# A hybrid block kernel: two weight loads on ScalarE's queue, a norm's sums one product earlier, weight sums stored by GpSimd, and a set VectorE order in the last half

## The chip, the cores and the metric

The kernel runs on one core of one Trainium2 chip. Time is device microseconds of one execution of the whole program, with all inputs and outputs in the chip's HBM. Lower is better. Before the change, three runs took 2157.55, 2159.38 and 2161.64 us; the median is 2159.38.

## What is computed

One residual block over a sequence of 2048 frames with 1024 channels, all in float32 (a depth of 1):

```python
def rmsnorm(x, g):
    return x * lax.rsqrt(jnp.mean(x * x, axis=-1, keepdims=True) + EPS) * g

def reference(x, ...):
    h = rmsnorm(x, norm_mix_pre)
    u_pool, u_glu, g_a, g_b = jnp.split(h @ w_in, [512, 1536, 2560], axis=-1)   # 1024 -> 3584
    branch_a = pool_mixer(u_pool, pool_w, pool_scale, w_pool_out)   # windows 2, 4, 8, 16; 512 -> 1024
    branch_b = conformer_conv(u_glu, conv_w, conv_b, ln_g, ln_b, w_conv_out)
    # GLU, causal depthwise conv of 31 taps, LayerNorm, swish, 512 -> 1024
    merged = sigmoid(g_a) * branch_a + sigmoid(g_b) * branch_b
    x = x + rmsnorm(merged @ w_o, norm_mix_post)
    h = rmsnorm(x, norm_mlp_pre)
    f = jnp.square(relu(h @ w_up)) @ w_down                          # 1024 -> 4096 -> 1024
    return x + rmsnorm(f, norm_mlp_post)
```

## The kernel before

**Layout and blocks.** Channels lie on the 128 partitions, frames on the free axis. The 2048 frames are two blocks of 1024 (`NB`), each of two halves of 512 frames (`T`); a tile of 128 x 1024 float32 (512 KB) holds one half for two groups of 128 channels. The stages run one after the other on TensorE: input projection of block 0 (`glu`, `pool`, `ga`, `gb`), branch A of block 0, the same for block 1, then merge and out-projection of block 0 (`wo`), branch A of block 1 (`A`), up-projection of block 0 (`up`), merge, out-projection and up-projection of block 1, and the down-projection of both blocks (`down`).

**Products.** A float32 product is made of three products in the format fp32r: weight and data are each split into a high part (ScalarE casts) and a low part (VectorE subtracts), and high x high, high x low and low x high are added in PSUM (`split`, L216; `split_w`, L223; `matmuls`, L265). On top of that, most projections use a scheme of seven block products instead of eight (`Octet`, L427). Its operands are sums and differences of weight tiles and of data tiles. `weight_parts` (L306) makes the weight sums on VectorE in tiles named `ws`, of which there are two buffers (L93). Both blocks need the same sums, so block 0 stores them to HBM and block 1 loads them back; `save` (L341) puts them on the list `due`, and `flush` (L253), called after every product, empties that list from its end through SP's queue. The low parts go on the list `later` and are stored one flush after.

**Queues.** `load` (L127) issues a DMA from SP, `aside` (L130) from GpSimd (POOL in the profile), `store` (L134) from ScalarE. Each engine issues its DMAs in order with its other instructions, and an issue waits, as any instruction does, for what it reads. Most loads, and the stores of `flush`, are on SP.

**What sets the order.** A scheduler orders each engine's instructions by priority and dependences. `high_priority` moves a group ahead by some number of places; `behind` (L171) ties a group behind the last marked instruction of its engine; a dependence of the kind `NOSYNC` fixes an order without a wait. Work beside the main line runs in generators (`Lane`), stepped after each product.

**Places that the change touches.**
- *The opening*, `first_half` (L826): the first x tile, the constants `cst`, the first weight tile `wr` in two halves, and the other x tiles, all issued by SP.
- *The norm of block 0's out-projection*: `out_proj` returns a generator `chain`. Its first step adds the halves of the sum of squares (`total`, L770) and sums over the partitions with eight matmuls against `inv_d` (`root_pe`, L617); its second computes the inverse root on VectorE (`root_dve`, L623) and its last spreads it over the partitions with matmuls (`spread_pe`, L719). `step` (L1754) takes these steps after the first, second and fourth product of branch A of block 1, each `behind` that product's marks. Branch A multiplies its products by the gates, which it loads from HBM (`sad`) into tiles `tr`.
- *The last norm of block 1's out-projection*: `out_proj_2` (L1370), `make` (L1377). The norm's product of a tile is a `mul` by the spread root `rb`, and the sum with x is stored as `x1d`.
- *The end*: the down-projection of the last half (block 1, half 0) in `at_end` (L1994). Its last unit is made in two quarters of 256 frames, so that the norm of the first lies beside the product of the second; `InOrder` (L152) fixes the order there as written. Sums (L2037) of the squares (`squared`, L2024), an inverse root (`root_short`, L665), its spread (L713) and the outputs follow; `idle` (L604) fills TensorE's time around the last sums with matmuls that nobody reads, `IDLE` (L61) of them. Beside it the half 0 of block 0 is finished by the generator `fin[0, 0].steps` (L1953): four scalings by `rb`, each followed by an accumulating load of `x1d` on GpSimd's queue (L1973), and then four outputs on the same queue. Its scalings carry the names `big<-big,rb`; two of the last half's final adds are done by GpSimd itself (L2104).

Of the kernel before, what the change touches and what calls it, by code (L numbers as in the profile page):

```python
# [57 lines left out]
ORDER = (1, 2, 6, 5, 7, 3, 4)  # L58
SEEDED = (1, 5, 6, 2, 7, 3, 4)

IDLE = (7, 5, 3)  # L61


def f32(ap):
    return ap.bitcast(F32)
# [3 lines left out]
def block_kernel(  # L69
# [41 lines left out]
    def two(ap):  # L111

        return ap.rearrange("p (c t) -> p c t", c=2)
# [7 lines left out]
    def sub(o, a, b):  # L121
        return nc.vector.tensor_tensor(o, a, b, op=ALU.subtract)  # L122

    def mul(o, a, b):
        return nc.vector.tensor_tensor(o, a, b, op=ALU.mult)

    def load(o, src):  # L127
        return nc.sync.dma_start(o, src)

    def aside(o, src):  # L130

        return nc.gpsimd.dma_start(o, src)
# [80 lines left out]
        return cst[:, i : i + 1]  # L213


    def split(src, pl, tag):  # L216
        hi = mk(pl, tag, F32R)
        lo = mk(pl, tag, F32R)
        nc.scalar.copy(hi, src)
        sub(lo, src, f32(hi))  # L220
        return hi, lo

    def split_w(src, n=TB, low=None, home=None):  # L223
# [82 lines left out]
    def weight_parts(src, key, b, keep, raw):  # L306


        s = {}

        def get(q):
            if q not in raw:
                raw[q] = mk(p_wr, "wr")
                load(raw[q], src[q])
            return raw[q]

        def minus(a, b, op=sub):
            o = mk(p_ws, "ws")
            op(o, a, b)
            return o  # L320

        def source(i):
            if i in (1, 2, 4):
                return get({1: 0, 2: 1, 4: 3}[i])
            if (key, i, "sum") in kept and b:
                if ("s", i) not in raw:
                    raw["s", i] = mk(p_wr, "wr")
                    load(raw["s", i], kept[key, i, "sum"])
                return raw["s", i]
            if i == 7:  # L330
                return minus(get(0), get(2))
            if i in (5, 6) and 1 not in s:
                s[1] = minus(get(2), get(3), add)
            if i == 6:
                s[2] = minus(s[1], get(0))
                return s[2]
            if i == 5:
                return s[1]
            return minus(get(1), s[2])

        def save(i, what, tile):  # L341
            kept[key, i, what] = dram("kept")
            (due if what == "sum" else later).append((kept[key, i, what], f32(tile)))

        def part(i):
            with tc.high_priority(offset=ahead[0]):
                for q in {1: (0,), 2: (1,), 4: (3,), 7: (0, 2), 5: (2, 3), 6: (2, 3, 0), 3: (1,)}[i]:
                    if (key, i, "sum") not in kept or not b:
                        get(q)
                if (key, i, "sum") in kept and b:  # L350
                    source(i)
            with tc.high_priority(offset=40):
                t = source(i)
                w = raw.pop(("w", i), None)
                if w is None and not ((key, i, "low") in kept and b):
                    w = split_w(t)
            if w is None:
                with tc.high_priority(offset=80):
                    w = split_w(t, low=kept[key, i, "low"])
            if keep and not b:  # L360
                save(i, "low", w[1])
                if keep == "sums" and i not in (1, 2, 4):
                    save(i, "sum", t)
            return w

        return part
# [459 lines left out]
    def first_half(o):  # L826

        with tc.high_priority(offset=URGENT):
            load_x(0, x0, ORDER_X[:1])
            load(cst, params)  # L830
            o.raw[0] = w = mk(p_wr, "wr")
            load(w[:, :T], w_in[0, 0, :, :T])
            load_x(0, x0, ORDER_X[1:2])
            load(w[:, T:], w_in[0, 0, :, T:])
            load_x(0, x0, ORDER_X[2:CPS])
            for q in (1, 2, 3):
                o.get(q)
            load_x(0, x0, ORDER_X[CPS:])
# [531 lines left out]
    def out_proj_2(b, cells, made):  # L1370
# [4 lines left out]
        ps, held = {}, {}  # L1375

        def make(c, t):  # L1377
            mul(two(o[c, t]), two(o[c, t]), per_token(rbs[t]))
            add(x[c, t], x[c, t], o[c, t])
            load(x1d[b, c, t], x[c, t])  # L1380
            gained(o[c, t], x[c, t], C_MPRE, c)
            return o[c, t]
# [370 lines left out]

    def step():  # L1754
        n[0] += 1
        if n[0] in (1, 2, 4):
            with behind():
                next(chain, None)
        if n[0] > 3:
            parts.step()  # L1760

    parts.need(2)
    branch_a(1, mixed, step)
    conv1.rate = 1.2
# [171 lines left out]
    class Finish:  # L1936


        def __init__(self, b, t):
            self.b, self.t, self.x, self.ready = b, t, {}, {}  # L1940
            self.order = (0, 1, 2, 3)

        def fetch(self, cells):
            for c in cells:
# [46 lines left out]
    HT = T // 2  # L1991
    HG = G // 2

    def at_end(f, w, cells):  # L1994

        o = 1
        k, c = (o, f.b), f.order[3]
# [21 lines left out]

        def joined(h):  # L2020
            of = ps[h][:, :T].rearrange("p (c t) -> p c t", c=2)
            add(at(y, h), at(y, h), of)

        def squared(h):  # L2024
            sq = mk(*FO)[:, :T].rearrange("p (c t) -> p c t", c=2)
            for i in (0, 1):
                nc.scalar.activation(sq[:, i], at(y, h)[:, i], AF.Square, scale=SQ)
            for i in (0, 1):
                nc.scalar.activation(
                    at(y, h)[:, i], at(y, h)[:, i], AF.Copy, scale=col(C_MPOST + 2 * c + i)  # L2030
                )
            return sq
# [33 lines left out]
        with tc.high_priority(offset=URGENT):  # L2066
            for s in range(SLABS):
                slab(0, s)
            joined(0)
            sq = squared(0)  # L2070
            at_1 = len(nc.cur_bb.bb.instructions)
            slab(1, 0)
# [7 lines left out]
            st = floor(0)  # L2080
            sums(0, before(0) + [sq[:, 0], sq[:, 1]], st, False, True)
            y0 = root(st)
            slab(1, 1)
            rbs[0] = spread_whole(y0)
            slab(1, 2)
# [4 lines left out]
                plus(0, n)  # L2090
            times(0, c)
            joined(1)
            plus(0, c)
            st = floor(1)
            sums(1, before(1), st, False, False)
            idle(IDLE[0], first[:, :T])
            sq = squared(1)
            sums(1, [sq[:, 0], sq[:, 1]], st, False, True)
            idle(IDLE[1], first[:, :T])
            rbs[1] = spread_whole(root(st))  # L2100
# [223 lines left out]
    for n, item in enumerate(items[:-SLABS]):  # L2324
# [23 lines left out]
        if item == PREPARE:  # L2348
            lanes.append(Lane(1.2, chain_of(level_weights(2, 1, fo), level_cells())))
        if (s, i, b) == (0, ALONE[0], 0):  # L2350
            lanes.append(Lane(3, fin[0, 0].steps(2, 150)))
        if n and (i in ALONE or b == 0 or (s, i) == FILL[:2]):
            w = [weight_down(i, s, o) for o in (0, 1)]
        here = split_of.pop(n)
# [13 lines left out]
    for n, (s, i, b) in enumerate(END):  # L2368
        if n == 0:
            acc[0, b] = psum("down")  # L2370
        end.append(coming.pop(0))
        product(acc[0, b], weight_down(i, s, 0), end[n], start=n == 0, stop=s == LAST)
        if n + 2 < SLABS:
            coming.append(token_cells(*END[n + 2]))
        w = [weight_down(i, n, 1, BIG)] if n == 0 else w + [weight_down(i, n, 1, BIG)]
        if s == LAST:
            last_product(i, 0, b, acc[0, b])
        bg()
    empty()
    at_end(fin[1, 0], w, end)  # L2380


# [66 lines left out]
```

## Time and profile before

| | |
|---|---|
| median of three runs | 2159.38 us |
| the profiled execution, its own time | 2157.5 us |
| its span, first to last instruction | 2155.7 us |
| mean clock granted to TensorE | 0.997 |
| TensorE busy | 2136.2 us, 9585 matmuls |
| VectorE, ScalarE, GpSimd busy | 1666.9, 1042.6, 78.2 us |
| DMA | 618.39 MB, 287 GB/s over the span |

Times within the profile are microseconds from the start of the span. A row of the timeline gives the start, the time, the engine, the line of the kernel, the operation, its output and inputs, and in brackets how long the engine stood idle before it and what ended that. A row of the view by windows gives, for one stretch, its length, the busy time and the number of instructions of PE, PEld, DVE, ACT and POOL, the clock granted to TensorE, the busy share of the DMA engines and GB/s. Matmuls overlap in a pipeline, so a matmul of 0.39 us is followed by the next one after less time than that.

### The profile page before, as it was taken

What the parts mean: (1) busy time and instruction counts of PE and PEld (TensorE: products, weight loads), DVE (VectorE), ACT (ScalarE), POOL (GpSimd) and SP (SyncE); (2) the same over time, 40 slices, a digit from 0 to 9 for tenths busy, and PEclk for the clock granted to TensorE, in tenths of its full rate; (3) what the DMA queues carried; (4) which work ended last, traced back from release to release, by engine and by line L of the source; (5) the groups of instructions that cost most, each with busy time, mean ns of one, the idle gap of its engine ahead of it and who ended that gap; (6) DMA issues with size and microseconds to landing.
All of it is one profiled execution on the core that took longest, in us unless ns stands there. A gap on an engine that the chain in (4) does not pass through costs nothing.

```text
span 2155.7 us, 25279 instructions
## 1 busy us (share of the span) xinstructions
PE 2136.2 (99%) x9585; PEld 1770.2 (82%) x9585; DVE 1666.9 (77%) x1635; ACT 1042.6 (48%) x1102; POOL 78.2 (4%) x143
## 2 busy tenths in 40 slices
PE   9999999999999999999999999999999999999997
PEld 7888888888888878888888888888888888888887
DVE  8998688997778878997768795667776657576975
ACT  6444454334543635545554684655663332234761
POOL 1000000000000000000000000000000000110002
PEclk9999999999999999999999999999999999999999
DMA  7688897778997777445698698677898997896967
GB/s 274 239 295 320 323 365 272 251 244 307 333 379 247 267 293 284 175 149 201 250 354 298 244 340 324 248 263 271 319 348 306 353 379 262 330 372 231 304 248 211
DMA packets 173929, 618.39 MB, mean 287 GB/s; under 512 B 19312, under 2 KB 21616, under 8 KB 173808
## 3 DMA queue, kind: packets, MB, share of 16 engines
q1 hardware_dynamic: 143168, 506.44, 64.6%
q0 software_dynamic: 17824, 64.07, 8.4%
q10 hardware_dynamic: 12816, 46.27, 5.3%
q8 instruction: 75, 1.23, 0.2%
q14 instruction: 46, 0.38, 0.0%
HBM read 406.89 MB, written 209.81 MB: 286 GB/s over the span
## 4 chain that ended last, share of the span: by engine, by line
PE 86%; DVE 7%; DMA 4%; issue 1%; ACT 0%; SPq 0%; DVEq 0%
PE up L269 23%; PE down L269 20%; PE wo L269 8%; PE gb L269 7%; PE ga L269 7%; PE glu L269 5%; PE rb L269 5%; PE B L269 4%; PE A L269 4%; PE pool L269 3%; DVE y L1012 1%; DVE big L122 1%; DVE wl L122 1%; DVE tr L119 1%; DVE tr L122 1%
## 5 line engine op out<-in xcount | busy, mean ns | idle before, releaser
L269 PE MATMUL up<-big,wh 128*128 128x512 f32 x1792 | 480.3, 390 | 2.1 <-ACT wh L226 0.9
L269 PEld LDWEIGHTS up<-big,wh 128*128 128x128 f32 x1792 | 335.9, 188 | 72.9 <-ACT wh L226 1.3
L226 ACT CAST wh<-wr 128x1024 fp32r<-128x1024 f32 x196 | 205.8, 1052 | 346.2 <-issue 79.6
L1012 DVE SCALAR_TENSOR_TENSOR y<-v,cst,y 128x1024 f32<-128x1024 f32 x240 | 307.2, 1280 | 3.0
L269 PE MATMUL down<-big,wh 128*128 128x512 f32 x872 | 294.9, 389 | 0.0
L226 ACT CAST wh<-ws 128x1024 fp32r<-128x1024 f32 x128 | 134.7, 1052 | 309.9 <-PE up L269 75.7
L269 PE MATMUL up<-big,wl 128*128 128x512 f32 x896 | 276.0, 389 | 0.0
L269 PE MATMUL down<-big,wl 128*128 128x512 f32 x688 | 212.1, 389 | 0.0
L122 DVE TENSOR_TENSOR wl<-ws,wh 128x1024 fp32r<-128x1024 f32 x120 | 146.5, 1221 | 74.3 <-ACT wh L226 74.1
L269 PE MATMUL down<-tr,wh 128*128 128x512 f32 x504 | 196.2, 389 | 0.5 <-DVE tr L122 0.5
L269 PEld LDWEIGHTS up<-big,wl 128*128 128x128 f32 x896 | 168.1, 188 | 34.8
L269 PEld LDWEIGHTS down<-big,wh 128*128 128x128 f32 x872 | 163.7, 188 | 33.9
L122 DVE TENSOR_TENSOR wl<-wr,wh 128x1024 fp32r<-128x1024 f32 (+1 forms) x121 | 146.1, 1210 | 25.2 <-ACT wh L226 21.3
L122 DVE TENSOR_TENSOR big<-big,big 128x1024 fp32r<-128x1024 f32 (+1 forms) x108 | 129.9, 1220 | 38.6 <-ACT big L1147 14.4
L269 PEld LDWEIGHTS down<-big,wl 128*128 128x128 f32 x688 | 129.2, 188 | 26.8
L122 DVE TENSOR_TENSOR tr<-tr,big 128x1024 fp32r<-128x1024 f32 x94 | 112.6, 1219 | 49.3 <-ACT big L1885 35.8
L269 PE MATMUL wo<-big,wh 128*128 128x512 f32 x480 | 128.6, 390 | 0.0
L269 PE MATMUL glu<-big,wh 128*128 128x512 f32 x464 | 126.2, 393 | 1.7 <-ACT wh L532 0.8
L269 PE MATMUL ga<-big,wh 128*128 128x512 f32 x448 | 120.1, 389 | 0.0
L269 PE MATMUL gb<-big,wh 128*128 128x512 f32 x448 | 120.0, 390 | 0.0
L1885 ACT CAST big<-tr 128x1024 fp32r<-128x1024 f32 x70 | 71.8, 1049 | 90.3 <-DMA tr<-fd 68.3
L269 PEld LDWEIGHTS down<-tr,wh 128*128 128x128 f32 x504 | 94.6, 188 | 20.5 <-DVE tr L122 1.0
(244 smaller groups left out, 3412.0 us busy)
## 6 DMA issues: line engine op xcount, KB each, us to landing
tr<-fd SPq DMA_DIRECT2D x98, 512.0 KB, 7.4
wl<-kept SPq DMA_DIRECT2D x85, 512.0 KB, 5.0
wr<-w_down SPq DMA_DIRECT2D x80, 512.0 KB, 7.5
kept<-wl SPq DMA_DIRECT2D x72, 512.0 KB, 5.9
wr<-w_up SPq DMA_DIRECT2D x64, 512.0 KB, 4.7
wr<-w_in SPq DMA_DIRECT2D x59, 512.0 KB, 5.7
fd<-tr ACTq DMA_DIRECT2D x54, 512.0 KB, 5.3
big<-fd SPq DMA_DIRECT2D x48, 512.0 KB, 6.4
```

Of the source, the lines that this page charges most:

```text
L119: return nc.vector.tensor_tensor(o, a, b, op=ALU.add)
L122: return nc.vector.tensor_tensor(o, a, b, op=ALU.subtract)
L226: nc.scalar.copy(hi[:, :n], src[:, :n])
L269: i = nc.tensor.matmul(ps, w[wp][:, (at + k) * P : (at + k + 1) * P], rhs[k][xp], start=start and n == 0, stop=stop and n == len(order) - ...
L1012: nc.vector.scalar_tensor_tensor(acc, v[:, k : k + TB], wk, acc, op0=ALU.mult, op1=ALU.add)
L1885: nc.scalar.copy(hi, t)
```

## The change

It has six parts. The constants and the two halves of the first weight are issued by ScalarE instead of SP. The sums of block 0's out-projection norm are tied behind the work before branch A's first product, and the spread follows the third product instead of the fourth. The weight sums are stored at once, by GpSimd. In `make`, the norm's product of the second tile in order is tied behind the last low part that was written. At the end, the finish of block 0's half 0 is stepped by hand: up to its root's spread ahead of `at_end`, two scalings after the first quarter's join, and the rest behind the first root. And around the last sums, the join is split in two, one of the two last squares moves from ScalarE to VectorE, a final add moves behind it, and four filler matmuls stand where seven stood.

```diff
-IDLE = (7, 5, 3)
+IDLE = (4, 5, 3)
...
+    last_low = []
+
     def split(src, pl, tag):
...
-        sub(lo, src, f32(hi))
+        last_low[:] = [sub(lo, src, f32(hi)).ins]
         return hi, lo
...
         def save(i, what, tile):
             kept[key, i, what] = dram("kept")
-            (due if what == "sum" else later).append((kept[key, i, what], f32(tile)))
+            if what == "sum":
+                aside(kept[key, i, what], tile)
+            else:
+                later.append((kept[key, i, what], f32(tile)))
...
             load_x(0, x0, ORDER_X[:1])
-            load(cst, params)
+            store(cst, params)
             o.raw[0] = w = mk(p_wr, "wr")
-            load(w[:, :T], w_in[0, 0, :, :T])
+            store(w[:, :T], w_in[0, 0, :, :T])
             load_x(0, x0, ORDER_X[1:2])
-            load(w[:, T:], w_in[0, 0, :, T:])
+            store(w[:, T:], w_in[0, 0, :, T:])
...
         def make(c, t):
-            mul(two(o[c, t]), two(o[c, t]), per_token(rbs[t]))
+            i = mul(two(o[c, t]), two(o[c, t]), per_token(rbs[t]))
+            if (c, t) == (0, 1):
+                tc.add_manual_dep(i.ins, last_low[0].name, NOSYNC, reason="in order")
...
     def step():
         n[0] += 1
-        if n[0] in (1, 2, 4):
+        if n[0] in (1, 3):
             with behind():
                 next(chain, None)
         if n[0] > 3:
             parts.step()
 
+    with behind():
+        next(chain, None)
     parts.need(2)
     branch_a(1, mixed, step)
...
-    def at_end(f, w, cells):
+    def at_end(f, w, cells, rest):
...
         def joined(h):
             of = ps[h][:, :T].rearrange("p (c t) -> p c t", c=2)
-            add(at(y, h), at(y, h), of)
+            if h == 0:
+                add(at(y, h), at(y, h), of)
+            else:
+                for i in (0, 1):
+                    add(at(y, h)[:, i], at(y, h)[:, i], of[:, i])
...
             for i in (0, 1):
-                nc.scalar.activation(sq[:, i], at(y, h)[:, i], AF.Square, scale=SQ)
+                if h == i == 1:
+                    z = at(y, h)[:, i]
+                    nc.vector.scalar_tensor_tensor(
+                        sq[:, i], z, SQ * SQ, z, op0=ALU.mult, op1=ALU.mult
+                    )
+                else:
+                    nc.scalar.activation(sq[:, i], at(y, h)[:, i], AF.Square, scale=SQ)
...
             joined(0)
+            next(rest, 0), next(rest, 0)
             sq = squared(0)
...
             y0 = root(st)
+            drain(rest)
             slab(1, 1)
...
             joined(1)
-            plus(0, c)
             st = floor(1)
             sums(1, before(1), st, False, False)
             idle(IDLE[0], first[:, :T])
             sq = squared(1)
+            plus(0, c)
             sums(1, [sq[:, 0], sq[:, 1]], st, False, True)
...
-            lanes.append(Lane(3, fin[0, 0].steps(2, 150)))
+            g00 = fin[0, 0].steps(2, 150)
+            lanes.append(Lane(3, g00))
...
         bg()
+    with behind():
+        while fin[0, 0].rb is None:
+            next(g00)
+    lanes[:] = [lane for lane in lanes if g00 not in lane.gens]
     empty()
-    at_end(fin[1, 0], w, end)
+    at_end(fin[1, 0], w, end, g00)
```

The order of instructions is decided by the scheduler, so the diff alone does not show it. Three places follow; a row gives the line, the operation, its output and inputs with the numbers of the tiles, and the shape.

First, VectorE around branch A's first gate products in block 1. `tr_5651` is the sum of squares of the out-projection's norm, `A_...` are branch A's products, `sa` begins the inverse root. Before:

```order
L119 TENSOR_TENSOR tr_5651<-tr_5651,tr_5946 128x1024
L122 TENSOR_TENSOR big_5960<-big_5489,big_5959 128x1024
L122 TENSOR_TENSOR big_5969<-big_5567,big_5968 128x1024
L125 TENSOR_TENSOR tr_5980<-A_5992,tr_5980 128x1024
L119 TENSOR_TENSOR tr_5651<-tr_5651 128x512
L125 TENSOR_TENSOR tr_5982<-A_6022,tr_5982 128x1024
L632 TENSOR_SCALAR sa_6054<-rb_6049 128x4
```

After:

```order
L119 TENSOR_TENSOR tr_5651<-tr_5651,tr_5946 128x1024
L119 TENSOR_TENSOR tr_5651<-tr_5651 128x512
L122 TENSOR_TENSOR big_5960<-big_5489,big_5959 128x1024
L122 TENSOR_TENSOR big_5969<-big_5567,big_5968 128x1024
L125 TENSOR_TENSOR tr_5981<-A_5993,tr_5981 128x1024
L637 TENSOR_SCALAR sa_6025<-rb_6020 128x4
```

The total of 128x512 moved ahead of two low parts and of the first gate product, right behind the last add; the inverse root now follows the first gate product instead of the second.

Second, VectorE in the last norm of block 1's out-projection, where `rb_9715` is the spread root, `big_9597` and `big_9606` are low parts of the up-projection's data, and `big_9489` to `big_9495` the sums with x:

```order
 L122 TENSOR_TENSOR big_9597<-big_9323,big_9596 128x1024
+L122 TENSOR_TENSOR big_9606<-big_9375,big_9605 128x1024
 L125 TENSOR_TENSOR big_9528<-big_9528,rb_9715 128x1024
-L122 TENSOR_TENSOR big_9606<-big_9375,big_9605 128x1024
+L125 TENSOR_TENSOR big_9584<-big_9584,rb_9715 128x1024
 L119 TENSOR_TENSOR big_9489<-big_9489,big_9528 128x1024
-L125 TENSOR_TENSOR big_9584<-big_9584,rb_9715 128x1024
-L125 TENSOR_TENSOR big_9438<-big_9438,rb_9715 128x1024
 L119 TENSOR_TENSOR big_9491<-big_9491,big_9584 128x1024
```

The second low part moved ahead of the norm's first product.

Third, the end of GpSimd's queue, with the accumulating loads (`big<-x1d`), the outputs of block 0's half 0 and GpSimd's two final adds. Before:

```order
L1973 DMA big_12190<-x1d_145 128x1024
L1973 DMA big_12697<-x1d_147 128x1024
L1973 DMA big_13786<-x1d_149 128x1024
L1973 DMA big_13814<-x1d_151 128x1024
L132 DMA out<-big_12190 128x1024
L132 DMA out<-big_12697 128x1024
L132 DMA out<-big_13786 128x1024
L132 DMA out<-big_13814 128x1024
L2104 TENSOR_TENSOR big_16108<-big_16108,big_12354 128x2x256
L2104 TENSOR_TENSOR big_16110<-big_16110,big_12437 128x2x256
```

After:

```order
L1982 DMA big_12190<-x1d_145 128x1024
L1982 DMA big_12697<-x1d_147 128x1024
L132 DMA out<-big_12190 128x1024
L1982 DMA big_13786<-x1d_149 128x1024
L1982 DMA big_13814<-x1d_151 128x1024
L132 DMA out<-big_12697 128x1024
L132 DMA out<-big_13786 128x1024
L132 DMA out<-big_13814 128x1024
L2125 TENSOR_TENSOR big_16108<-big_16108,big_12354 128x2x256
L2125 TENSOR_TENSOR big_16110<-big_16110,big_12437 128x2x256
```

The first output moved ahead of the third and fourth load; the final adds stand last in both.

More of the change, by code (lines that the diff above doesn't have):

```diff
@@ L1940, in __init__ @@
             self.b, self.t, self.x, self.ready = b, t, {}, {}
-            self.order = (0, 1, 2, 3)
+            self.order, self.rb = (0, 1, 2, 3), None
         def fetch(self, cells):
```

## Prediction

> **What bounds the kernel now.** I read the page first: the busy times, and the chain that ended last.
>
> ```profile
> PE 2136.2 (99%) x9585; PEld 1770.2 (82%) x9585; DVE 1666.9 (77%) x1635; ACT 1042.6 (48%) x1102; POOL 78.2 (4%) x143
> PE 86%; DVE 7%; DMA 4%; issue 1%; ACT 0%; SPq 0%; DVEq 0%
> ```
>
> TensorE is busy for all but 19.5 us of a span of 2155.7. No matmul goes away, so only those 19.5 us, and stretches at a lower clock, can be won. Next the waits of TensorE (for whom; total, times, longest; here and below, rows that the argument doesn't use are left out between those shown).
>
> ```profile
> PE rb L596 <- DVE tr L119: 2.9, 1, 2.9
> PE rb L713 <- DVE sy L674: 1.4, 2, 0.9
> PE up L269 <- ACT wh L226: 0.9, 1, 0.9
> PE glu L269 <- ACT wh L532: 0.8, 1, 0.8
> PE glu L269 <- DVE big L122: 0.2, 1, 0.2
> ```
>
> Two more, of 0.8 and 0.5 us, are quoted below; the rest of the 19.5 lies mostly before the first matmul and after the last. I followed each of these waits in the timeline, since the edits touch most of them.
>
> **The norm's sums (largest term).** Out-projection of block 0 ends at 749 and branch A of block 1 begins.
>
> ```profile
> 751.11 1.23 DVE L119 TENSOR_TENSOR tr<-tr,tr 128x1024 f32<-128x1024 f32 x1 [4.10 <-ACT tr L764]
> 754.58 0.39 PE L269 MATMUL A<-big,wh 128*128 128x512 f32 x1
> 761.11 1.22 DVE L125 TENSOR_TENSOR tr<-A,tr 128x1024 f32<-128x1024 f32 x1 [5.55 <-DMA tr<-sad]
> 762.26 0.68 DVE L119 TENSOR_TENSOR tr<-tr 128x512 f32<-128x512 f32 x1
> 764.14 0.16 DVE L632 TENSOR_SCALAR sa<-rb 128x4 f32<-128x4 f32 x1
> 766.12 0.16 DVE L122 TENSOR_TENSOR sq<-sy,sp 128x4 fp32r<-128x4 f32 x1
> 763.08 1.02 PE L596 MATMUL rb<-inv_d,tr 128*128 128x1 f32 x8 [2.91 <-DVE tr L119]
> 764.98:768.40 3.42, 3.42 (x10) 2.67 (x9) 1.09 (x7) 0.00 (x0) 0.00 (x0) 0.51 1.03 408
> ```
>
> The total (762.26) needs only the add of 751.11, but stands behind the gate product of 761.11, which waits 5.55 us for a load. TensorE therefore sits 2.91 us, and then runs at a clock of 0.51 (seventh figure of the last row) for 3.42 us: 3.42 x 0.49 = 1.7 lost. Now the total stands right behind its add, so it is done near 752.3 + 0.7 = 753.0; the sums stand one product earlier, where TensorE begins the second A product at 754.58. Margin 1.6 us. Gain: 2.9 + 1.7 = **4.6**. What is late next is the broadcast, one product earlier as well: the inverse root still follows the gate product (761.11 + 1.2), takes 2.1 us (from 764.14 to the end of the operation at 766.12, 11 small operations), so 764.4. A product takes from 754.58 to 763.08 - 2.91 = 760.17, 5.6 us, and the eight sums 1.0, so TensorE comes to the broadcast at 754.58 + 1.0 + 11.2 = 766.8. Margin 2.4.
>
> The Trainium skill ("TensorE: Matmul & The Clock Gate", What's actually happening) gives the half clock to an idle window of about 3.4 us. A gap of 2.91 would then not have caused it, and the sum would be 1.7 smaller; the row with 0.51 straight behind the gap speaks against that.
>
> **Weight sums stored by GpSimd.** 24 stores of 512 KB leave SP's queue, where they stood behind the product's flush, last in first out.
>
> ```profile
> 834.82 1.22 DVE L122 TENSOR_TENSOR ws<-ws,wr 128x1024 f32<-128x1024 f32 x1
> 848.86 1.39 PE L269 MATMUL up<-big,wh 128*128 128x512 f32 x5 [0.48 <-DVE tr L119]
> 830.00:870.00 40.00, 38.65 (x170) 31.37 (x169) 33.04 (x30) 20.40 (x21) 0.00 (x0) 1.00 0.69 244
> 855.42 0.42 SPq L128 DMA_DIRECT2D kept<-ws  x1
> 863.97 1.23 DVE L122 TENSOR_TENSOR ws<-wr,ws 128x1024 f32<-128x1024 f32 x1 [5.81 <-DMA kept<-ws]
> 865.23 1.05 ACT L226 CAST wh<-ws 128x1024 fp32r<-128x1024 f32 x1 [4.16 <-DVE ws L122]
> 866.33 0.97 PE L269 MATMUL up<-big,wh 128*128 128x512 f32 x3 [0.87 <-ACT wh L226]
> ```
>
> The sum of 834.82 is stored only at 855.42, and VectorE waits 5.81 us for its buffer; through the cast that reaches TensorE as 0.87 us. GpSimd is idle there (fifth pair of the row by windows, 0.00), so the store starts near 836 and would have to land 20 us late to matter. Gain **0.9**. The 0.48 at 848.86 stays: the order on VectorE in front of that evacuation is unchanged, and TensorE waits for it alone (bounds 0 and 0.6 won). Each issue on GpSimd cost 0.53 us in this row of like stores:
>
> ```profile
> L132 POOL DMA_DIRECT2D x1d<-big x8 | 4.3, 534 | 131.2 <-DVE big L119 131.2
> ```
>
> The Trainium skill ("SBUF — State Buffer", SBUF: two separate sides) warns that GpSimd cannot write a DMA's descriptors while VectorE runs an operation that holds the port they share, which speaks against this edit. If each of the 24 stores met one operation of 1.2 us, an estimate by that page is 29 us of lateness spread over them; here the issues took 0.53 beside a busy VectorE, and none is on the path, so the sum stays.
>
> **Fixed VectorE order in block 1's last norm.**
>
> ```profile
> 1249.58 1.22 DVE L125 TENSOR_TENSOR big<-big,rb 128x1024 f32<-128x1024 f32 x1 [0.34 <-PE rb L725]
> 1250.71 1.22 DVE L122 TENSOR_TENSOR big<-big,big 128x1024 fp32r<-128x1024 f32 x1
> 1251.98 0.50 PE L269 MATMUL up<-big,wh 128*128 128x512 f32 x1 [0.77 <-DVE big L122]
> ```
>
> The norm's product (1249.58) now follows the low part (1250.71) instead of leading it. The low part starts some 1.1 us sooner and ends at 1250.8; TensorE wants it at 1251.2. Gain **0.8**. The norm's products are 1.1 later; nothing on TensorE waited for them after this.
>
> **The opening.** The constants and the first weight leave SP's queue for ScalarE's, ahead of the first activation.
>
> ```profile
> 2.12 0.43 SPq L128 DMA_DIRECT2D big<-xt  x1
> 4.67 1.34 ACT L806 ACTIVATE big<-big,cst 128x512 fp32r<-128x512 f32 x2 [2.44 <-DMA cst<-params]
> 16.00:55.00 39.00, 38.97 (x187) 32.17 (x185) 37.52 (x59) 26.53 (x29) 5.95 (x12) 1.00 0.69 255
> 7.27 0.62 ACT L532 CAST wh<-wr 128x512 fp32r<-128x512 f32 x1 [1.26 <-DMA wr<-w_in]
> ```
>
> The two issues ahead of the second x tile (2.12) go, 2 x 0.43 = 0.9 us sooner; the third ahead of later tiles makes 1.3. The weight no longer lands behind two x tiles in one queue, so the 1.26 us of ScalarE shrink. Three issues of 0.43 delay ScalarE by 1.3; it was idle for 2.44 us before 4.67, so that is covered. But VectorE is then busy for 37.52 of 39 us (the row by windows), and TensorE waits only 0.2 for it at the end of that; this chain moves only as the x tiles do, and the bytes ahead of those stay the same. Bounds: -0.4 (two queues share the bandwidth, the first x tile lands one issue later) to 1.3 (all the issue time); I take **0.5**, between them.
>
> **The end.** Here three edits meet.
>
> ```profile
> 2134.45 0.68 PE L713 MATMUL rb<-ident,sy 128*128 128x128 f32 x4 [0.95 <-DVE sy L674]
> 2141.30 1.86 PE L607 MATMUL rb<-ones 128*128 128x512 f32 x7
> 2141.63 0.73 ACT L2027 ACTIVATE fo<-big 128x256 f32<-128x256 f32 x2 [11.60 <-DVE big L119]
> 2143.00 0.95 PE L2037 MATMUL rb<-inv_d,fo 128*128 128x1 f32 x8
> ```
>
> Two scalings of 1.2 us move behind the first root: the 0.95 goes. Later, squares are ready at 2141.63 + 0.73 = 2142.36, but the sums start at 2143.00, behind 7 filler matmuls of (2143.00 - 2141.30) / 7 = 0.24; with 4 fillers they end at 2142.3, and one square on VectorE (about 0.35, half of the 0.68 at 762.26) makes the squares as early. So the sums start near 2142.3, and the last root is 0.95 + 0.7 = 1.7 earlier. But the moved scalings feed GpSimd's accumulating loads, and its queue now holds an output behind the second one:
>
> ```profile
> 2130.02 0.90 POOL L1973 DMA_DIRECT2D big<-x1d  x1 [13.47 <-DVE big L125]
> 2135.74 0.88 POOL L1973 DMA_DIRECT2D big<-x1d  x1 [2.36 <-issue]
> 2145.19 0.53 POOL L132 DMA_DIRECT2D out<-big  x1 [2.65 <-DVE s L125]
> 2147.19 2.49 POOL L2104 TENSOR_TENSOR big<-big,big 128x512 f32<-128x512 f32 x2 [1.47 <-issue]
> big<-x1d POOLq DMA_DIRECT2D x4, 512.0 KB, 7.8
> ```
>
> The first output must wait for its load to land (2130.02 + up to 7.8), near 2136; then come loads three and four, near 2136.5 and 2137.5, the last 1.8 later than 2135.74. As long as now behind it (2145.19 - 2135.74 = 9.45), the last output goes out near 2147, and behind the other output's bytes, up to 2147.5. GpSimd's two final adds (2147.19) stand behind it: start between 2148.0 (an issue of 0.53 later) and 2149.5 (with the 1.47 before them now), 0.8 to 2.3 late. I take **1.0 lost**, nearer the first, since the 1.47 was no wait for anything named. The last outputs wait for those adds, whatever the root does. Bounds: 1.7 won (the queue keeps up) to 2.3 lost.
>
> **Sum.** 4.6 + 0.9 + 0.8 + 0.5 - 1.0 = 5.8 us off the profiled execution's 2157.5 (span 2155.7): 2151.7. The median of the runs, 2159.4, is 1.9 above that execution, so it gives **2153.6**.
>
> **Rivals.** *Tail keeps up* (0.10): the adds are not late, 1.7 won instead of 1.0 lost: 2150.9. For it: fewer loads compete while the first two land. Against: GpSimd's queue is in order. *The wait moves* (0.13): the gate's load (5.55 us at 761.11) lands more than 2.4 us later, or the earlier TensorE meets another load; up to the 2.9 come back: 2156.5. For it: that load was already late. *Nothing in the middle* (0.07): TensorE is held at the sums all the same, by another input of theirs: 2153.6 + 4.6 = 2158.2. Against: the order shows the total right behind its add. *Sums block VectorE* (0.08): in the up-projection after 800 weight sums now stand ahead of two PSUM evacuations.
>
> ```profile
> 812.90 1.22 DVE L119 TENSOR_TENSOR ws<-wr,wr 128x1024 f32<-128x1024 f32 x1 [0.55 <-DMA wr<-w_up]
> ```
>
> Such a sum waits for its weight's load. The evacuation at 848.86 had no lead on TensorE, so where one stands behind two sums (2.4 us) and a load later by as much as the worst here (5.55), TensorE stops for up to 8.0 us and then runs 3.4 us at half clock (1.7). From 5.8 + 4.3 = 10.1 us lost in the two places together the change is slower; both at their full price, 19.4: 2173.0. Against: VectorE has 7 us of idle time in the 40 of 830 to 870.
>
> **Chances.** Forecast 0.62. About 0.2% (4.3 us) is what a measurement here can tell from no change. Faster: 0.62 + 0.10 + 0.02 of the moved wait = 0.74; same: 0.11 + 0.07 = 0.18; slower 0.08. The range takes in the unknown bounds downward (tail 2.7, opening 0.8, the evacuation 0.6, and about 1 for the spread of the runs) and the moved wait upward: 2148.5 to 2157.
>
> **What would show it.** Right: no wait of TensorE at the sums near 760 and no clock of 0.5 behind it; no VectorE wait on `kept<-ws` near 860; no wait near 1250 or at the first root of the end; GpSimd's final adds as far from the last matmul as now, or farther. Wrong: a new wait of TensorE on `up`, a wait at the broadcast after the third A product, or the adds 2 us sooner against the last root.

## The result and the profile after

| | before | changed |
|---|---|---|
| median of 20 runs | 2158.99 us (2155.90 to 2161.64) | 2162.0 us (2158.70 to 2166.88, and one of 3614.52) |
| profiled execution, its own time | 2157.5 us | 2163.86 us |
| its span | 2155.7 us | 2161.8 us |

The ratio is 1.0015, with a 95% interval of 1.0008 to 1.0022: the change costs 3 us where a gain of 5.8 was forecast, and the median lies above the stated range. (The run at 3614.52 us, with a mean granted clock of 0.555 where the others have 0.997 to 0.999, stays out of the ratio.)

The page of the changed kernel has the same busy times, but another chain, in the same order of figures as before:

```profile
PE 2135.2 (99%) x9582; PEld 1767.8 (82%) x9582; DVE 1668.0 (77%) x1637; ACT 1040.8 (48%) x1101; POOL 91.0 (4%) x167
PE 70%; issue 19%; DVE 5%; DMA 3%; POOL 1%; ACT 1%; POOLq 0%; ACTq 0%; SPq 0%; DVEq 0%
```

GpSimd's 24 new issues are there (143 to 167 instructions). The waits of TensorE (for whom; total, times, longest) tell more:

```profile
PE up L271 <- ACT tr L446: 2.3, 1, 2.3
PE up L271 <- DVE big L122: 1.9, 2, 1.1
PE up L271 <- DVE tr L119: 1.8, 2, 1.6
PE ga L271 <- ACT wh L228: 1.5, 1, 1.5
PE gb L271 <- ACT tr L446: 1.3, 1, 1.3
PE pool L271 <- DVE tr L119: 1.2, 2, 0.9
...
PE rb L718 <- DVE sy L679: 0.4, 1, 0.4
```

The wait of 2.9 at the norm's sums is gone, and of the waits for the roots at the end 0.4 is left of 1.4. But there are new waits that the forecast has nowhere: 1.5 before `ga`, 0.9 before `pool`, 1.3 before `gb`, and some 6 us in `up`, where 2.2 stood. The norm's sums in the timeline, with the row by windows of the stretch that had a clock of 0.51 before:

```profile
759.70 0.95 PE L601 MATMUL rb<-inv_d,tr 128*128 128x1 f32 x8
764.98:768.40 3.42, 3.42 (x17) 2.84 (x16) 2.36 (x9) 1.05 (x1) 0.00 (x0) 1.00 1.02 416
```

No bracket, so no wait, and a clock of 1.00: this step did what was forecast. Around 142, first two rows of the kernel before, then those of the changed kernel:

```profile
128.59 1.06 ACT L764 ACTIVATE tr<-tr 128x1024 f32<-128x1024 f32 x1 [2.37 <-DMA tr<-xt]
138.35 1.21 DVE L122 TENSOR_TENSOR ws<-ws,wr 128x1024 f32<-128x1024 f32 x1
```

```profile
133.34 1.06 ACT L769 ACTIVATE tr<-tr 128x1024 f32<-128x1024 f32 x1 [6.21 <-DMA tr<-xt]
134.44 1.23 DVE L119 TENSOR_TENSOR tr<-tr,tr 128x1024 f32<-128x1024 f32 x1 [3.01 <-ACT tr L769]
140.24 1.22 DVE L122 TENSOR_TENSOR ws<-ws,wr 128x1024 f32<-128x1024 f32 x1
141.49 1.04 ACT L228 CAST wh<-ws 128x1024 fp32r<-128x1024 f32 x1 [4.56 <-DVE ws L122]
142.59 1.65 PE L271 MATMUL ga<-big,wh 128*128 128x512 f32 x6 [1.50 <-ACT wh L228]
```

Around 870, in the changed kernel:

```profile
858.16 0.53 POOL L132 DMA_DIRECT2D kept<-ws  x1 [17.92 <-DVE ws L122]
867.77 1.23 DVE L122 TENSOR_TENSOR ws<-wr,ws 128x1024 f32<-128x1024 f32 x1 [6.36 <-issue]
869.03 1.04 ACT L228 CAST wh<-ws 128x1024 fp32r<-128x1024 f32 x1 [8.22 <-DVE ws L122]
869.98 1.00 ACT L446 COPY tr<-up 128x1024 f32<-128x1024 f32 x1
871.04 1.66 PE L271 MATMUL up<-big,wh 128*128 128x512 f32 x6 [2.32 <-ACT tr L446]
```

At 142 a load of x (`tr<-xt`) comes late; ScalarE waits 6.21 us for it where it waited 2.37, VectorE 3.01 behind that, and the weight sum that `ga` needs is late (140.24 against 138.35). At 870 VectorE waits 6.36 us for a buffer of `ws`, as it did before the change (5.81): the row says only "issue", but in the trace the store of 858.16 landed at 867.69, 0.08 us before the sum. ScalarE now has the cast of that sum ahead of a PSUM evacuation (the copy of a product out of PSUM, at 869.98), so TensorE waits 2.32 instead of 0.87.

SP's queue before and after, up to that late load:

```profile
121.06 0.33 SPq L128 DMA_DIRECT2D wr<-w_in  x1
121.45 0.45 SPq L128 DMA_DIRECT2D kept<-ws  x1
121.95 0.42 SPq L128 DMA_DIRECT2D tr<-xt  x1
124.53 0.32 SPq L128 DMA_DIRECT2D kept<-wl  x1
124.95 0.49 SPq L128 DMA_DIRECT2D tr<-xt  x1
129.20 0.81 SPq L128 DMA_DIRECT2D wr<-w_in  x2
```

```profile
120.87 2.83 SPq L128 DMA_DIRECT2D wr<-w_in  x3
123.75 0.70 SPq L128 DMA_DIRECT2D tr<-xt  x1
125.59 0.33 SPq L128 DMA_DIRECT2D kept<-wl  x1
126.02 0.86 SPq L128 DMA_DIRECT2D tr<-xt  x1
```

With the store gone from this queue, the scheduler put two weight loads, which stood behind both x loads, ahead of them (x3 at 120.87). The diff moves only a store; the loads moved with it.

### The profile page after: what moved, and what is told of

Its sections match the earlier page's. It is cut to its first block, busy times and chain, and to the rows that moved or that the text cites. A ratio compares the mean times of both kernels' runs of the same rounds, so it can differ in the third digit from the quotient of the medians.

```text
span 2161.8 us, 25300 instructions
## 1 busy us (share of the span) xinstructions
PE 2135.2 (99%) x9582; PEld 1767.8 (82%) x9582; DVE 1668.0 (77%) x1637; ACT 1040.8 (48%) x1101; POOL 91.0 (4%) x167
## 4 chain that ended last, share of the span: by engine, by line
PE 70%; issue 19%; DVE 5%; DMA 3%; POOL 1%; ACT 1%; POOLq 0%; ACTq 0%; SPq 0%; DVEq 0%
PE up L271 24%; PE down L271 21%; PE rb L271 4%; PE gb L271 4%; PE B L271 4%; PE ga L271 4%; PE wo L271 3%; PE glu L271 3%; PE A L271 2%; DVE y L1017 1%; DMA big<-x1d 1%; PE pool L271 1%; DVE tr L119 1%; DVE big L122 1%; DMA kept<-ws 1%
```

## The experiments

**Theory S:** the move of the stores costs, by what it does to the order or to the queues. **Rival O:** the opening shifts the work of VectorE against the loads. From the first four runs on, theory S split in two: **Q**, GpSimd's queue itself (its stores take bandwidth beside SP's loads), and **O**, the order that the scheduler makes without them on SP (this O is not the opening). Ratios are to the kernel before, run beside it on the same chip.

**e1**, the stores back on SP, all else kept.

```diff
-            if what == "sum":
-                aside(kept[key, i, what], tile)
-            else:
-                later.append((kept[key, i, what], f32(tile)))
+            (due if what == "sum" else later).append((kept[key, i, what], f32(tile)))
```

> The changed kernel with the weight sums stored as before (list, flush, SP's queue); all other parts of the change kept. Theory S: moving these 24 stores is what costs, since the waits that are new in the changed kernel between 130 and 610 us (1.5 + 1.3 + 1.2 us and smaller) and between 837 and 877 us (2.3 + 1.6 + 1.1) all lie where weight sums are made; without it the time is near 2151 to 2153, and TensorE waits for neither wh at 142 nor tr at 870. Rival O: the new opening shifts VectorE's work against the loads, and the waits up to 610 us come from it; then this run still has them and gives 2158 to 2160.

Measured: 2155.03 us, 0.9985 (0.9976 to 0.9994). Both waits around 145 are gone, and `up` waits for no ScalarE copy. Theory S; without this one part the change is a gain of some 3 us, less than the expected 2151 to 2153.

**e2**, this edit alone, on the kernel before (the same lines, the other way round).

> The kernel before with nothing but the weight sums stored at once by GpSimd. Theory S: 7 to 11 us slower than before, 2166 to 2170, with the new waits near 142, 249, 604 and 840 to 877 us. Rival O: within 2 us of before, 2157 to 2161, and the waits up to 610 us are absent.

Measured: 2165.96 us, 1.0035 (1.0021 to 1.0048), the largest loss of all, with the wait for `wh` of 1.5 in place. Its opening is the old one, so the opening is not the cause.

**e3**, the changed kernel with the stores issued at once, by SP.

```diff
-                aside(kept[key, i, what], tile)
+                load(kept[key, i, what], f32(tile))
```

> The changed kernel with the weight sums stored at once, as in the change, but issued by SP. It keeps the place of the stores in the program and takes away GpSimd's queue. If the place and the order that the scheduler makes of it cost (the order on VectorE is nearly that of the changed kernel), the time is like the changed kernel's, 2160 to 2164. If GpSimd's queue costs (later landing, or loads that pass the stores on SP), it is near 2152 to 2155.

Measured: 2155.76 us, 0.9990 (0.9981 to 0.9999). "At once" is not the cause. My expectation said that VectorE's order is nearly the changed kernel's; that was wrong. Apart from the stores, the trace shows the operations of SP, VectorE and ScalarE in the order of e1. So the run left Q and O both open.

**e4**, only the norm's sums and spread sooner, on the kernel before.

```diff
-        if n[0] in (1, 2, 4):
+        if n[0] in (1, 3):
...
+    with behind():
+        next(chain, None)
     parts.need(2)
```

> The kernel before with nothing but the sums of the norm taken one product earlier and its spread one product earlier. The prediction's 4.6 us (2.9 of wait and 1.7 of half clock) give 2154 to 2155, with no wait at the sums near 760 us. If the wait only moves to the broadcast or to a gate, 2157 to 2159.

Measured: 2155.23 us, 0.9989 (0.9980 to 0.9997): a gain, but half of what was forecast. In its timeline, the place where VectorE loses its lead, and what TensorE pays later:

```profile
810.41 1.23 DVE L119 TENSOR_TENSOR ws<-wr,wr 128x1024 f32<-128x1024 f32 x1 [5.67 <-DMA wr<-w_up]
811.55 1.22 DVE L119 TENSOR_TENSOR tr<-up,tr 128x1024 f32<-128x1024 f32 x1
848.57 1.62 PE L269 MATMUL up<-big,wh 128*128 128x512 f32 x6 [1.59 <-DVE tr L119]
```

Where VectorE waited 0.55 us for a weight (812.90 before), it now waits 5.67, with an evacuation behind the sum; the wait of TensorE at 848 grows from 0.48 to 1.59.

**e5**, the changed kernel, stores on GpSimd, with the order of SP, VectorE and ScalarE fixed to that of e1 by dependences without a wait (three long lists of places).

```diff
+    for e, order in (("SP", SP_ORDER), ("DVE", DVE_ORDER), ("Activation", ACTIVATION_ORDER)):
+        e = getattr(mybir.EngineType, e)
+        own = [i for i in nc.cur_bb.bb.instructions if i.engine == e]
+        for p, q in zip(order, order[1:]):
+            tc.add_manual_dep(own[q], own[p].name, NOSYNC, reason="in order")
```

> The changed kernel, its weight sums stored at once by GpSimd, but with the instructions of SP, VectorE and ScalarE held in the order that they have in e1 (2155.0). What is left of the difference is the queue. Theory Q (GpSimd's stores run beside SP's loads as a second stream and take their share of the DMA engines, where on SP they stood in line behind them): 2160 to 2164, with the loads around a store as slow as in the changed kernel (x and weight loads of 9 us near 122). Theory O (the scheduler, seeing SP free of the stores, puts two weight loads ahead of two x loads near 122 and sums ahead of evacuations near 830): the time is e1's, 2154 to 2157, and x lands in 6 to 7 us.

Measured: 2155.67 us, 0.9989 (0.9981 to 0.9998). The order costs, not the queue. By the traces, the operations of the three engines follow each other as in e1; in the changed kernel they do not, on SP near 75, 125, 270 and 820 us, on VectorE near 85, from 120 to 143 and from 868 to 904, and on ScalarE near 128 and from 860 to 881. The waits of TensorE in e5, the first four rows:

```profile
PE up L496 <- DVE tr L344: 1.6, 1, 1.6
PE rb L837 <- POOL inv_d L412: 1.0, 1, 1.0
PE up L496 <- DVE big L347: 1.0, 2, 0.8
PE up L496 <- ACT wh L453: 0.9, 1, 0.9
```

No wait before `ga` is left, and none for a ScalarE copy in `up`; the 1.6 for the evacuation at 848 stays, as in e4.

**e9**, the mirror: stores on SP through the list, all else in the changed kernel's order (the same loop, other lists, the 24 stores left free).

> The mirror of e5: the weight sums stored by SP as before (list and flush), but with the instructions of SP, VectorE and ScalarE otherwise held in the order that they have in the changed kernel. Theory O (the order costs, not the queue): slow like the changed kernel, 2160 to 2164, with two weight loads ahead of two x loads near 122 us. Theory Q': it is the order together with GpSimd's separate stream that costs; then 2155 to 2158.

Measured: 2159.54 us, 1.0011 (1.0002 to 1.0020). Against e1, which differs from it only in this order, that is 0.26% slower, some 5.6 of the 6.5 us that lie between e1 and the changed kernel (0.30%). It fell just short of the lower end that was expected for the order. What is left, 0.04% here and between e5 and e1, is inside the intervals, so a small share of the queue is neither shown nor excluded.

**e10**, e5 with only SP's order fixed.

```diff
+    for a, b in zip(SP_ORDER, SP_ORDER[1:]):
+        tc.add_manual_dep(on_sp[b], on_sp[a].name, NOSYNC, reason="in order")
```

> The changed kernel with GpSimd's stores, and SP's instructions alone held in the order of e1; VectorE and ScalarE are left to the scheduler, which still puts two weight sums ahead of two evacuations near 830 and of a sum of squares near 125. If SP's order of loads is the cause, 2154 to 2157 as in e5. If VectorE's order is, 2160 to 2163.

Measured: 2159.70 us, 1.0007 (0.9998 to 1.0015): between the two expected ranges, nearer to that of VectorE's order. In its profile the wait before `ga` is 0.72 and none follows before `pool`, but all those in `up` are there.

```profile
872.26 1.67 PE L331 MATMUL up<-big,wh 128*128 128x512 f32 x6 [2.28 <-ACT tr L506]
878.50 1.63 PE L331 MATMUL up<-big,wh 128*128 128x512 f32 x6 [0.47 <-DVE tr L175]
```

So SP's order goes with most of the waits around 145, and that of VectorE and ScalarE with those around 870. The split is not a clean one: with SP held, VectorE and ScalarE took an order between 280 and 320 us that is neither e1's nor the changed kernel's. The intervals of e5, e10 and the changed kernel touch, so the split in us is the profiles', not the times'.

**e6**, e1 with e4's edit undone; **e8**, e1 with block 0's evacuations in `up` at a higher priority:

```diff
-                    mark(add(o, ps, s))
+                    with tc.high_priority(offset=100) if not b else nullcontext():
+                        mark(add(o, ps, s))
```

> e1 without the norm's sums being taken sooner: what is left of the change is the opening, the set VectorE order and the end. If the parts add up, e1's 2155.0 loses the 2.2 that e4 won: 2157 to 2158, like before. If the opening and the end win on their own, 2155 to 2156; if they cost and the sums win more in their company, 2159 to 2160.

> e1 with the PSUM evacuations of block 0's up-projection moved ahead of the weight work on VectorE, about two places. If VectorE's order there gives back what the sums won (waits of TensorE of 1.5 us for the evacuation near 848), that wait goes and the time is 2153 to 2154. If the weight loads set the pace there, the wait moves to the weights' casts or low parts and the time stays 2155 to 2156.

Measured: e6 2158.0 us, 0.9999 (0.9990 to 1.0008). The sums won 0.14% over it in e1, 3.0 us, though the two intervals just meet, and the other parts together nothing that can be told. e8: 2157.31 us, 0.9991 (0.9982 to 1.0001), no gain: the 1.6 at 848 went, and a wait of 2.8 us for a weight's cast (`up<-ACT wh`) came. Ahead of that cast VectorE stood idle for 6.25 us until the store of a `ws` buffer had landed (863.31), which the evacuations' place does not touch: the weights set the pace there.

**e7**, e1 with GpSimd's instructions at the end in written order.

```diff
-            mybir.EngineType.PE, mybir.EngineType.DVE, mybir.EngineType.Activation
+            mybir.EngineType.PE, mybir.EngineType.DVE, mybir.EngineType.Activation,
+            mybir.EngineType.Pool,
```

> e1 with GpSimd's instructions at the end in the order in which they are written: all four accumulating loads, then the four outputs, then the adds. By the prediction's step on the end (the output ahead of the third load makes the adds 0.8 to 2.3 late) the adds start 1 to 2 us sooner after the first accumulating load (17 us instead of 18.3), and the time is 0.7 to 1.5 under e1's: 2153.5 to 2154.3. If the loads are bound by the DMA engines whatever the order, the adds stay where they are: 2155.

Measured: 2155.16 us, 0.9988 (0.9978 to 0.9997), no different from e1 in time. First and last rows of the tail on GpSimd, in the changed kernel and in e7:

```profile
2135.88 0.89 POOL L1982 DMA_DIRECT2D big<-x1d  x1 [13.56 <-DVE big L125]
2142.40 1.76 POOL L1982 DMA_DIRECT2D big<-x1d  x2
2154.24 2.48 POOL L2125 TENSOR_TENSOR big<-big,big 128x512 f32<-128x512 f32 x2
```

```profile
2129.47 0.90 POOL L1979 DMA_DIRECT2D big<-x1d  x1 [13.53 <-DVE big L125]
2145.29 2.50 POOL L2123 TENSOR_TENSOR big<-big,big 128x512 f32<-128x512 f32 x2
```

From the first load to the adds: 18.4 us in the changed kernel, 17.2 before the change (2130.02 to 2147.19), 15.8 in e7. The output ahead of the third load costs the adds what was forecast; taking it away moves them 2.5 us against e1 (18.3), and the end of the span by 1.2 (counted from 2120) in these two profiles, of which the times show nothing.

**e11, e12**, both kernels once more, for a second profile.

> The kernel before once more, for a second profile of the same program. The prediction priced the wait at the norm's sums from one execution: 2.9 us and 1.7 us of half clock. If that price is the program's own, it is seen again; if it hangs on how the waits fall in one execution, the wait is 2 to 2.5 us and the half clock behind it may be missing, and the stretch of half clock near 11 us may be missing too.

> The changed kernel once more, for a second profile of the same program. The waits that are the program's own come back: for wh near 142 us (1.5), after weight sums near 838 to 877 us (about 5 in all), and none at the norm's sums near 760. Waits that are not seen again belong to one execution.

Measured, single runs: 2154.73 and 2161.37 us. The changed kernel's waits came back (`ga` 1.50, `pool` 0.88, in `up` 1.51, 1.6 and 1.1), except the 1.3 before `gb`. The kernel before, again, at the norm's sums, and its clock behind them by windows; then e2's clock, whose wait there was 2.4:

```profile
763.34 1.02 PE L596 MATMUL rb<-inv_d,tr 128*128 128x1 f32 x8 [2.23 <-DVE tr L119]
766.60:770.00 3.40, 3.40 (x16) 2.81 (x15) 0.07 (x2) 0.00 (x0) 0.00 (x0) 1.00 1.01 402
```

```profile
768.25:771.67 3.42, 3.42 (x10) 2.65 (x8) 1.09 (x7) 0.00 (x0) 0.00 (x0) 0.51 1.01 394
```

The wait is the program's; its size and the half clock behind it are the execution's: 2.9 us with half clock, 2.4 (e2) with, 2.2 (e11) and 2.1 (e6) without. The half clock near 11 us in the first profile was in no other run.

The Trainium skill ("TensorE: Matmul & The Clock Gate", What's actually happening) states that the window in which idleness counts is about 3.4 us and runs free of the kernel. The stretches at half clock are 3.4 us long here too, but the gaps ahead of them are shorter. If the eight small sums (1.0 us) counted as idle, the gaps would be 3.9 and 3.4 with half clock, and 3.2 and 3.1 without. Against that stands a wait in e8 that has no small sums behind it, with the row by windows of the half clock that followed:

```profile
865.75 2.21 PE L271 MATMUL up<-big,wh 128*128 128x512 f32 x6 [2.75 <-ACT wh L228]
866.60:870.00 3.40, 3.40 (x10) 2.63 (x9) 3.40 (x4) 1.73 (x3) 0.00 (x0) 0.51 0.97 365
```

Half clock also followed a wait of 1.94 in e2 (`up`, 872.79) and one of 0.92 with eight small sums in e10 (247.83), and none followed those of 2.32 in the changed kernel and 2.28 in e10. So the prediction's reading stands, that a gap of 2.91 can be followed by half clock; what decides it is open.

**All runs by stage.** The same matmul's start, minus its start in the first profile of the kernel before (us, from the timelines):

```
                        134    155    600    778    830    880   2120   2138
before again (e11)     -0.1   -0.1   +0.9   -1.3   -1.4   -2.0   -1.9   -2.5
changed                -0.7   +2.5   +5.1   +0.4   +0.4   +5.2   +5.2   +4.5
changed again (e12)    -1.1   +2.5   +3.4   -1.1   -1.1   +3.5   +3.7   +2.6
e1 stores on SP        -0.7   -0.7   +1.0   -3.7   -3.6   -0.2   +0.1   -0.9
e5 order of e1         -1.1   -1.1   +0.6   -4.1   -4.1   -2.5   -2.2   -3.4
e9 order of the change -0.8   +1.3   +2.5   -2.2   -2.2   +0.6   +0.3   -0.9
e4 only the sums       -0.2   +1.1   +2.5   -2.2   -2.2   -1.5   -1.5   -1.6
e2 only the stores     -0.7   +2.7   +3.8   +3.3   +3.3   +8.1   +9.3   +9.8
e3 SP at once          -0.7   -0.7   -0.6   -5.2   -3.6   -1.6   -1.2   -2.3
e7 end in order        -0.8   -0.4   +2.1   -2.6   -2.6   -1.8   -0.0   -1.2
e8 evacuations first   -1.0   -0.7   +0.4   -4.3   -3.7   +1.1   +2.2   +1.0
e10 SP order of e1     -1.1   -0.1   +5.0   +0.3   +1.1   +6.7   +7.7   +6.5
e6 without the sums    -0.9   -0.9   -0.3   -2.7   -2.7   -2.1   -1.6   -2.8
```

Read by differences along a row. From 134 to 155 the changed kernel loses 3.2 and 3.6 and e2 3.4, e1 and e5 nothing. From 830 to 880 the changed kernel loses 4.8 and 4.6, e2 4.8 and e10 5.6, e9 2.8; e1 3.4, e5 1.6 and e7 0.8, whose orders there are the same, so some 2.6 us of that is scatter; e4 0.7, and e6, without the sums, 0.6. (e8's 4.8 and e2's hold a stretch of half clock each.) From 155 to 600 the kernels lose 0.1 to 2.6 (before again 1.0), which is one execution against another; e10 loses 5.1, with a wait of 1.32 for a load and its half clock in it.

## Why the prediction was wrong, step by step

- **The step that failed: "Weight sums stored by GpSimd. Gain 0.9", with "none is on the path".** Measured, this edit costs 0.30% between e1 and the changed kernel, 6.5 us, and 0.35% alone (e2). Two things in the step were wrong. First, I paired rows badly: the sum of 834.82 was not the one stored at 855.42. These rows of the kernel before show it:

```profile
830.69 5.70 SPq L128 DMA_DIRECT2D kept<-ws  x2
834.82 1.22 DVE L122 TENSOR_TENSOR ws<-ws,wr 128x1024 f32<-128x1024 f32 x1
853.29 1.22 DVE L122 TENSOR_TENSOR ws<-wr,wr 128x1024 f32<-128x1024 f32 x1
```

  The store of 834.82's sum is the second of the two of 830.69, issued at 836.07. The one of 855.42 belongs to the sum of 853.29 and was issued 0.9 us after its end; it landed at 863.88, 8.5 us later, in a stretch in which the DMA engines were busy for 96% of the time. A store issued sooner had little to win there: GpSimd issued it 0.4 us after the sum's end, it landed 9.5 us later, and the changed kernel waits 6.36 us where 5.81 stood. Second, I priced only the moved instruction. Taking 24 stores off SP's queue let the scheduler reorder the loads behind them, and with them the weight sums on VectorE and the casts on ScalarE. e5 (order undone, GpSimd kept: 0.9989) and e9 (order kept, SP kept: 1.0011) show that the order is the cause. The listing of the order showed the moved sums before the run; I gave them a chance of 0.08 as the rival *Sums block VectorE*, in the up-projection alone. That rival is what happened there, at 1 to 4 us beyond e1, e5 and e7 instead of 19, and with ScalarE's copy rather than VectorE's evacuation as the worst wait. The loads of x around 122, worth 3.2 to 3.6, I had not looked at.
- **The norm's sums, 4.6.** The mechanism was right: no wait, no half clock, and the broadcast was not late. The size was off: alone it won 0.11% (e4) and in company 0.14% (e1 against e6), 2.4 and 3.0 us. Two parts of the term were too large. The wait of 2.9 with half clock is the dearest of four executions of it, 2.1 without half clock the cheapest: from 600 to 778 the changed kernel wins 4.7 on the first profile of the kernel before, and 2.4 on the second. And part of the lead is given back in `up`, where VectorE waits for weights (5.67 at 810.41 in e4) and TensorE then for VectorE (1.59). The prediction had that wait stay at 0.48, because the order just ahead of it is unchanged; but by e4's rows VectorE loses its lead earlier, at 810, where a weight sum now stands ahead of an evacuation.
- **The fixed VectorE order, 0.8.** The wait near 1252 went, but I wrote that nothing on TensorE waited for the later products. Something did, a low part that VectorE now made later:

```profile
1273.57 0.50 PE L271 MATMUL up<-big,wh 128*128 128x512 f32 x1 [0.79 <-DVE big L122]
```

  This row of the changed kernel takes the gain back 20 us later; the net is 0.
- **The opening, 0.5.** At 134 the kernels with the old opening stand at 0, -0.1 and -0.2 (e2: -0.7), those with the new one at -0.7 to -1.1. Some 0.5, as forecast, though e2's row shows that one execution's scatter is as large.
- **The end, 1.0 lost.** The wait at the first root is gone (0.95 in the first profile of the kernel before, 0.32 in the second), and the adds came 1.2 us later after the first load, as worked out. What that is worth at the end can't be told: from 2120 to the end of the span the changed kernel loses 0.8 against the first profile of before and e1 0.8, but e5 wins 0.7 and e9 0.8, and so does the kernel before, again (0.9), and the changed kernel's second profile neither wins nor loses more than 0.2. The forecast is inside that scatter.
- **The range** had no term for a reordering of unrelated work, though the change alters what the scheduler sees on a queue in two stages. That, not the single terms, put the time outside it: with the order held, e5's ratio makes 2156.6 of the 2158.99, inside the range.

The best of these kernels in the times, e1, e4, e5 and e7, are within 0.05% of each other, which can't be told apart, and beat both the kernel before (0.9985 to 0.9989) and the changed one.

**Open:** which of the moved rows on VectorE and ScalarE around 830 to 880 costs most was not tried one by one, nor the reason why the scheduler took two weight loads forward; that it then sees SP as free sooner is only argued. Nor was it tried whether a fifth weight buffer would keep the lead that the sums win.

## What to carry to other kernels

Moving a DMA to another queue is an edit of the order of everything that a scheduler places on the old queue; compare the order of all engines before and after, and price the moved loads, not only the moved store. If such a part is wanted, hold the rest of the order in place: the same 24 stores cost 6.5 us with a free order and nothing that could be told with a held one. And before pricing a wait, pair the row that waits with the very instruction that it waits for, and take its size from more than one execution.

## What was not expected of the hardware

- GpSimd issued its 24 stores beside a busy VectorE at 0.53 to 0.54 us each, in the changed kernel and in e5, and with the order held the kernel is no slower for them: no sign here of the delay that the Trainium skill ("SBUF — State Buffer", SBUF: two separate sides) warns of. The Trainium skill ties that delay to VectorE operations in a 2-port mode; whether any of those ran beside these issues, no trace here shows.
- With the same instructions in the same order, stages differ by 1 to 2.6 us from one execution to the next: e1 lost 3.4 us from 830 to 880, e7 0.8; e4 lost 1.3 us between 134 and 155, where the kernel before, in that order up to 749, lost nothing in two profiles.
- Half clock for 3.4 us followed idle gaps of TensorE of 2.4 and 2.9 us at the norm's sums, in two of four executions with such a gap, and elsewhere gaps of 2.75 (e8), 1.94 (e2) and 0.92 us (e10), but not two of 2.3 (the changed kernel and e10). The length of the gap alone does not decide it.
